# A seven-product output projection on one Trainium2 core: side work tied to the matmuls, and the two-group product moved to the end

## The chip, the cores and the metric

The kernel runs on one core of a Trainium2 chip. The metric is device microseconds of one execution, the median of several. The engines are named as the profile names them: PE (matmuls) and PEld (its weight loads), DVE (the vector engine), ACT (the scalar engine), POOL (GpSimd) and SP (which only starts transfers). A name with a q (SPq, ACTq) is the engine's instruction queue. Each engine executes its own list of instructions strictly in the order in which the program was laid out, and waits at an instruction whose inputs are not there yet.

## The reference, cut to what matters

One step of a layer with two kinds of attention heads, for 1024 prompt frames and 8 x 16 sample frames. All is float32.

```python
h = rms_norm(x, norm_pre)
q_sb, k_sb, v_sb, gate_sb, q_r, k_r, v_r, gate_r = project(h, w_in, pos)   # 2048 -> 8 x 1024
o_sb = stick_breaking_block(q_sb, k_sb, v_sb)        # 8 heads, strictly causal
o_r  = retention(q_r, k_r, v_r)                      # 8 heads, chunks of 64
y   = concat(head_norm(o_sb) * silu(gate_sb), head_norm(o_r) * silu(gate_r))
out = einsum('bte,ed->btd', y, w_out)                # 2048 x 2048
x   = x + rms_norm(out, norm_post)
```

## The kernel before, in words

**Precision.** A float32 matmul is made of three passes over operands that are split in a high part (rounded, by ACT) and a low part (the rest, by DVE). The helper `split` (L163) does that: L164 is its ACT instruction, L165 its DVE instruction. Weights go this way too: `wr` (as loaded) becomes `wh` and `wl`, 128 x 512 at a time. There are 5 buffers of `wr` and 4 of each half, so the splitting can run a few tiles ahead of PE.

**Order.** The program is written as nested loops over products, and between the matmuls `tick()` runs one step of one of a list of waiting generators (`Job`). A generator says with each `yield` how many ticks must pass before its next step. That fixes a program order. A scheduler then lays out each engine's list: it may pull an instruction ahead of the place where it was written when its model of the machine sees the engine free and the inputs ready. A helper `tied` (L186) keeps some instructions of the attention from being pulled ahead of the last projection matmul written before them (`anchor`): it adds a dependency that only the scheduler sees, with no wait on the chip.

**Stage 1 and 2.** The rows are handled in two groups: group 0 is four prompt tiles of 128 frames and the sample tile, group 1 the other four prompt tiles. For each group the kernel projects head after head (matmuls at L338 and L394, weights loaded at L327 and L380), and the attention of earlier heads runs between these matmuls. In the stick-breaking attention the weight rows `kp` and `be` of a tile go through a scan (L618), a product (L619), a turn through device memory (`s_be`), and a block transpose on DVE (L679), before PE multiplies them with the values (L719).

**The output projection** follows a seven-product scheme (Strassen's in Winograd's form) with 2 x 2 blocks of `w_out` and of `y`. Some products need sums of blocks. The function `sums` (L259) makes them: it loads a block of 4 x 256 columns into `br` (two buffers; two transfers, L249 or L257), does four DVE instructions (L274), and stores it from the ACT queue (L277), as `s_b` for the weights (32 items) and as `s_s` for the rows (8 items for each group). Between the steps of an item stand 4, 4, 4, 4 + 6 and 36 ticks, and the load of an item is written one whole item ahead. The 32 weight items and the 8 items of group 0's rows are started in group 1's first head, and are drained near its end; the rows of group 1 follow in the third stage.

**Stage 3.** `product(n, nh, groups, sample, ticks)` multiplies the left operand `mine[g, n]` of each group g by one half (nh) of the right block n: for each of 8 k it loads and splits a weight tile (L1142) and does three matmuls (L1127, L1128, L1129) for each accumulator `a`, two accumulators (tiles of 128 frames) a group. `left` (L282) prepares an operand: per k a load `yr` and a split into `mh`, `ml` (group 0) or `ah`, `al` (group 1). `collect` (L1179, L1181, L1177) adds a finished product to the areas `mh2`, `ml2`, `mh3`, `ml3` (group 0) and `out0` to `out3` (group 1) by the table GOES. An entry with a 1 at its end completes a block: `complete` then squares it (ACT, L1223) and multiplies it by `gpost` (DVE, L1230). After its four blocks a tile is finished by `finish`: the residual rows `xr` are loaded (L1243), the scale is computed (L236, L172 to L178: small DVE instructions and one square root on ACT), and each 512 columns are scaled and added (DVE at L1253, or ACT at L1250 and POOL at L1251) and stored (L1256).

The products before are, in this order: 5 and 3 for group 0 and the sample; 1, 2, 6, 7, 4 for both groups; 5 and 3 for group 1 alone. The last half product (3, group 1) is cut: the last 5 of its 8 k are multiplied tile after tile, from kept weights `mh2`, `ml2` (L1318), so that the first tile's finishing can start under the second tile's matmuls.

Of the kernel before, what the change touches and what calls it, by code (L numbers as in the profile page):

```python
# [16 lines left out]
P = 128  # L17
# [57 lines left out]
        1: ((C21, None, "+", 0),), 2: ((C11, C21, "+", 1),), 6: ((C12, C21, "+", 0),), 7: ((C22, C12, "+", 0),),  # L75
        4: ((C21, C22, "-", 1),), 5: ((C22, C22, "+", 1), (C12, C12, "+", 0)), 3: ((C12, C12, "+", 1),),
# [14 lines left out]
def tile_hybrid_step(  # L91
# [71 lines left out]
    def split(hi, lo, src):  # L163
        nc.scalar.activation(hi, src, AF.Copy)  # L164
        nc.vector.tensor_tensor(lo, src, hi.bitcast(F32), ALU.subtract)  # L165

    def inv_rms(pool, ssq, n, name):
# [11 lines left out]
        return r  # L179

# [62 lines left out]
    def sum_weights(k, c):  # L243
        cs = slice(c * 256, (c + 1) * 256)

        def load(r):
            for kk in range(2):
                rows = w_out[0, (kk * HT + k) * P : (kk * HT + k + 1) * P, :]
                nc.sync.dma_start(r[:, 2 * kk : 2 * kk + 2], rows.rearrange("p (a n) -> p a n", a=2)[:, :, cs])  # L249
# [4 lines left out]
    def sum_rows(gi, h):  # L254
        def load(r):
            for kk in range(2):
                nc.sync.dma_start(r[:, 2 * kk : 2 * kk + 2].rearrange("p a n -> p (a n)"), s_y[gi][kk * H + h][:, :512])  # L257
# [4 lines left out]
    def sums(pool, items):  # L262
# [8 lines left out]
        for i, (_, ops, dst) in enumerate(items):  # L271
            nxt = fetch(items[i + 1][0]) if i + 1 < len(items) else None
            for o, a, b, how in ops:
                nc.vector.tensor_tensor(r[:, o], r[:, a], r[:, b], ALU.add if how == "a" else ALU.subtract)  # L274
                yield D_SUM2[0]
            yield D_SUM2[1]
            nc.scalar.dma_start(dst, r)  # L277
# [3 lines left out]
    def left(gi, n, hi, lo, bufs, tag, deep):  # L281
# [3 lines left out]
        def load(h):  # L285
            r = bufs.tile([P, 256], F32, name=tag, tag=tag, bufs=deep)
            if src[0] == "y":
                nc.sync.dma_start(r, s_y[gi][src[1] * H + h][:, src[2] * 256 : src[2] * 256 + 256])
            else:
                nc.sync.dma_start(r, s_s[gi][h][:, src[1], :])  # L290
# [5 lines left out]
        for h in range(HT):  # L296
# [3 lines left out]
            split(hi[:, h], lo[:, h], r)  # L300
            yield D_OP

    def left_sample(kk, hi, lo, bufs, tag, deep):
        raw = []

        def load(h):
            r = bufs.tile([P, P], F32, name=tag, tag=tag, bufs=deep)
            nc.sync.dma_start(r, s_y[0][kk * H + h][:, 4 * P : 5 * P])
# [5 lines left out]
        for h in range(HT):  # L314
            if h + deep - 1 < HT:
                load(h + deep - 1)
            split(hi[:, h], lo[:, h], raw.pop(0))
# [90 lines left out]
    with ExitStack() as s1:  # L408
# [716 lines left out]
        def times(a, x, k, ts, wh, wl, first, last):  # L1125
# [3 lines left out]
            nc.tensor.matmul(a, lo[:, k, ts], wh, start=False, stop=last)  # L1129
# [69 lines left out]
    with ExitStack() as s3:  # L1199
# [5 lines left out]
        for c in range(4):  # L1205
            nc.scalar.dma_start(
                gpost[:, c * 512 : (c + 1) * 512], norm_post[0, c * 512 : (c + 1) * 512].partition_broadcast(P)
            )
# [10 lines left out]
        def square(key, c, o):  # L1219
# [3 lines left out]
            nc.scalar.activation(sq, o, AF.Square, accum_out=ssqs[key][0][:, c : c + 1])  # L1223
            ssqs[key][1].append(c)

        def complete(key, c):
# [3 lines left out]
            nc.vector.tensor_tensor(o, o, gpost[:, c * 512 : (c + 1) * 512], ALU.mult)  # L1230
# [8 lines left out]
        def load_rows(key):  # L1239
            xr = []  # L1240
            for a in range(2):
                xr.append(xp[0].tile([P, HALF], F32, name="xr", tag="xr", bufs=4))
                nc.sync.dma_start(xr[a], x_rows(tile_of(key))[:, a * HALF : (a + 1) * HALF])  # L1243
            return xr

        def scaled(key, c, rs, xr, pool, o=None):
            o = area(key, c) if o is None else o
            x = xr[c // 2][:, (c % 2) * 512 : (c % 2 + 1) * 512]
            if pool:
                nc.scalar.activation(o, o, AF.Copy, scale=rs)  # L1250
                nc.gpsimd.tensor_tensor(o, o, x, ALU.add)  # L1251
            else:
                nc.vector.scalar_tensor_tensor(o, o, rs, x, ALU.mult, ALU.add)  # L1253
# [17 lines left out]
        def both(n, i):  # L1271
            jobs_of = []
            mine[0, n] = operand(mp, (f"mh{i % 2}", f"ml{i % 2}"), 256)
            mine[1, n] = operand(c3, ("ah", "al"), 256, bufs=2)
            return [Job(left(g, n, *mine[g, n], rp, "yr", 4), D_OP) for g in (0, 1)]

        ready = [Job(left_sample(kk, *mine["s", kk], fp, "ys", 4), 1) for kk in (1, 0)]
        Job(collect(3, 0, product(3, 0, (0,), False, 1)), 1)
        for job in ready:
            drain(job)  # L1280
        ready = both(1, 0)
        Job(collect(3, 1, product(3, 1, (0,), True, 1)), 1)
        Job(collect(3, 0, product(3, 0, (), True, 2)), 1)
# [159 lines left out]
```

## Time and profile before

| | |
|---|---|
| median of 3 runs | 2404.86 us (2402.67 to 2405.93) |
| the profiled execution: its time | 2398.02 us |
| its span | 2396.3 us |
| PE busy | 2287.5 us (95%) |
| DVE, ACT, POOL busy | 1262.3, 927.8, 365.3 us |
| mean granted clock of PE | 0.984 |
| sums (L274) run | from 1177.7 us, until group 0's and the weights' are done near 1491 us |
| stage 3, first matmul to last | 1994.4 to 2376.0 us |

Matmuls are pipelined: one of 128 x 512 shows 0.39 us, but they start 0.23 us apart. PE's busy time therefore hides short waits, and the count of matmuls in a stretch of time says more. "Idle" in a row is the time in which an engine stood before that instruction, and the name behind the arrow is what ended it.

### The profile page before, as it was taken

How to read it: one execution, taken by the hardware profiler on the slowest of the kernel's cores; microseconds unless marked ns; L12 is line 12 of the kernel's file. 1: busy time of each engine (PE TensorE's matmuls, PEld its weight loads, DVE VectorE, ACT ScalarE, POOL GpSimd, SP SyncE). 2: the span in 40 equal slices, each digit the busy share in tenths (PEclk: the TensorE clock that was granted, in tenths of full speed). 3: DMA queues.
4: the chain of work that ended last, by engine and by line, in shares of the span. 5: the costliest groups of instructions: out<-in, count | busy, mean ns of one | idle time of the engine just before them, and what ended most of it. 6: DMA issues, size and time to landing. Idle time of an engine off the chain costs nothing. (4 is left out here: it accounts for less than half of the span.)

```text
span 2396.3 us, 39509 instructions
## 1 busy us (share of the span) xinstructions
PE 2287.5 (95%) x14496; PEld 2053.5 (86%) x14496; DVE 1262.3 (53%) x2580; ACT 927.8 (39%) x1968; POOL 365.3 (15%) x590
## 2 busy tenths in 40 slices
PE   7999999999999999999987979999999999899995
PEld 7999999999999999998876858888888887688884
DVE  7235444443535443455556565555454556655767
ACT  6324333333333333334332323343344445533443
POOL 3002020301112120202020201120211311000102
PEclk9999999999999999999998989999999999999998
DMA  7546666575756656776788888645555556774747
GB/s 249 192 145 177 191 177 200 168 220 157 215 177 183 197 148 191 200 234 206 221 257 249 253 248 260 160 134 153 156 150 145 159 155 163 247 244 159 240 135 251
DMA packets 448194, 465.24 MB, mean 194 GB/s; under 512 B 182144, under 2 KB 311168, under 8 KB 446848
## 3 DMA queue, kind: packets, MB, share of 16 engines
q1 hardware_dynamic: 321568, 305.92, 43.5%
q10 hardware_dynamic: 101344, 85.48, 11.0%
q0 software_dynamic: 25088, 71.33, 9.9%
q8 instruction: 113, 1.85, 0.3%
q14 instruction: 81, 0.66, 0.1%
HBM read 357.74 MB, written 104.86 MB: 193 GB/s over the span
## 5 line engine op out<-in xcount | busy, mean ns | idle before, releaser
L338 PE MATMUL acc<-mh,wl 128*128 128x256 f32 (+2 forms) x2304 | 659.0, 339 | 11.0 <-DVE wl L165 11.0
L338 PE MATMUL acc<-mh,wh 128*128 128x256 f32 (+2 forms) x2304 | 664.9, 341 | 0.8 <-DVE rk L431 0.7
L338 PE MATMUL acc<-ml,wh 128*128 128x256 f32 (+2 forms) x2304 | 663.3, 341 | 0.0
L165 DVE TENSOR_TENSOR wl<-wr,wh 128x512 fp32r<-128x512 f32 x531 | 366.7, 695 | 458.0 <-ACT wh L164 438.6
L164 ACT ACTIVATE wh<-wr 128x512 fp32r<-128x512 f32 x531 | 332.0, 630 | 660.4 <-PE acc L338 296.4
L338 PEld LDWEIGHTS acc<-mh,wl 128*128 128x128 f32 x2304 | 425.7, 189 | 41.1 <-DVE wl L165 13.6
L338 PEld LDWEIGHTS acc<-mh,wh 128*128 128x128 f32 x2304 | 421.6, 189 | 34.4 <-issue 3.3
L338 PEld LDWEIGHTS acc<-ml,wh 128*128 128x128 f32 x2304 | 423.3, 189 | 31.3 <-issue 3.3
L394 PE MATMUL accn<-whn,mh 128*128 128x256 f32 x1152 | 330.1, 287 | 0.0
L394 PE MATMUL accn<-wln,mh 128*128 128x256 f32 x1152 | 326.2, 283 | 0.3 <-DVE wln L165 0.3
L394 PE MATMUL accn<-whn,ml 128*128 128x256 f32 x1152 | 325.6, 283 | 0.0
L394 PEld LDWEIGHTS accn<-whn,mh 128*128 128x128 f32 x1152 | 221.0, 192 | 3.4 <-issue 1.1
L394 PEld LDWEIGHTS accn<-wln,mh 128*128 128x128 f32 x1152 | 221.1, 192 | 1.3 <-DVE wln L165 0.5
L394 PEld LDWEIGHTS accn<-whn,ml 128*128 128x128 f32 x1152 | 220.8, 192 | 0.0
L165 DVE TENSOR_TENSOR wln<-wrn,whn 128x512 fp32r<-128x512 f32 x128 | 88.0, 689 | 146.2 <-ACT whn L164 145.8
L164 ACT ACTIVATE whn<-wrn 128x512 fp32r<-128x512 f32 x128 | 80.7, 633 | 189.9 <-PE accn L394 87.7
L274 DVE TENSOR_TENSOR br<-br 128x256 f32<-128x256 f32 x192 | 79.0, 423 | 106.6 <-DMA br<-w_out 72.7
L582 POOL DMA_DIRECT2D be<-s_be x128 | 94.1, 742 | 133.7 <-DMA s_be<-be 115.1
L607 POOL TENSOR_SCALAR_AFFINE_SELECT kb<-kb 128x128 f32<-128x128 f32 x64 | 30.7, 488 | 455.7 <-ACT kb L601 453.5
L618 DVE TENSOR_TENSOR_SCAN kp<-kp 128x1152 f32<-128x1152 f32 (+4 forms) x40 | 82.3, 2058 | 33.4 <-POOL kp L607 16.8
L745 POOL DMA_DIRECT2D kcT<-cache_k x64 | 34.9, 547 | 422.6 <-PE pd L822 268.5
L1127 PE MATMUL a<-wh,mh 128*128 128x512 f32 x224 | 88.2, 399 | 7.9 <-ACT wh L164 7.9
(230 smaller groups left out, 3053.1 us busy)
## 6 DMA issues: line engine op xcount, KB each, us to landing
wr<-w_cols SPq DMA_DIRECT2D x384, 256.0 KB, 3.9
wrn<-w_rows SPq DMA_DIRECT2D x128, 256.0 KB, 3.2
kcT<-cache_k POOLq DMA_DIRECT2D x64, 512.0 KB, 8.0
vc<-cache_v SPq DMA_DIRECT2D x64, 512.0 KB, 5.5
wr<-s_b SPq DMA_DIRECT2D x80, 256.0 KB, 3.5
wr<-w_out SPq DMA_DIRECT2D x72, 256.0 KB, 4.3
br<-w_out SPq DMA_DIRECT2D x64, 256.0 KB, 5.2
s_b<-br ACTq DMA_DIRECT2D x32, 512.0 KB, 5.2
```

The source lines that it names most:

```text
L164: nc.scalar.activation(hi, src, AF.Copy)
L165: nc.vector.tensor_tensor(lo, src, hi.bitcast(F32), ALU.subtract)
L274: nc.vector.tensor_tensor(r[:, o], r[:, a], r[:, b], ALU.add if how == "a" else ALU.subtract)
L338: last = nc.tensor.matmul(a[:, :m], lhs[:, j, :], rhs[w][:, j, o : o + m], start=(w == 0 and j == 0 and n == 0), stop=(w == KT // WQ - 1 a ...
L394: anchor[0] = nc.tensor.matmul(a, lhs[q][:, jj, ts], rhs[:, j, :], start=(w == 0 and j == 0 and n == 0 and t % 2 == 0), stop=(w == KT // 2 ...
L582: q.dma_start(raw[32 * i : 32 * i + 32, :].rearrange("p (k a) -> p k a", a=32), s[:, :, 32 * i : 32 * i + 32].rearrange("k (j b) a -> b (k ...
L607: nc.gpsimd.affine_select(blk, blk, pattern=[[-1, P]], base=0, channel_multiplier=1, compare_op=ALU.is_gt, fill=fill,)
L618: nc.vector.tensor_tensor_scan(rev, rev, rev, 1.0, ALU.mult, ALU.bypass)
L745: ready.append((kc, nc.gpsimd.dma_start(kc, cache_k[h, m // 4, m % 4])))
L1127: nc.tensor.matmul(a, hi[:, k, ts], wh, start=first, stop=False)
```

## The change

- A new helper `pin` does for any instruction what `tied` does, in all stages: the scheduler may not lay it out ahead of the matmul last written. It is put on the loads, DVE instructions and stores of `sums`, on the loads and splits of `left` and `left_sample`, and in stage 3 on squares, the multiplication by `gpost`, the loads of `xr` and the DVE and ACT part of the scaling. The matmuls of `times` in stage 3 now set `anchor`, so the pins follow them. The loads and splits of weights, the additions of `collect` and the small instructions of the scale are not pinned.
- `gpost` is loaded from POOL's queue by a generator in place of ACT's queue at the start of stage 3.
- The products' order is 5 and 3 (group 0, sample), 1, 2, 6, 7 (both), 5 and 3 (group 1), then 4 (both). GOES for group 1 follows: product 7 now also writes C21, and 4 subtracts from C21. That adds four DVE additions of 128 x 512.
- The cut last half product is now that of 4 with its four accumulators: four tiles are finished at the end, two of each group, in place of two. `og` has two buffers in place of one, `xr` six in place of four; in this tail one of four column blocks of a tile goes by ACT and POOL, as before.
- The sample's operands are prepared at two places (one ahead of each half of product 3) in place of both at once.

```diff
     1: {
-        1: ((C21, None, "+", 0),), 2: ((C11, C21, "+", 1),), 6: ((C12, C21, "+", 0),), 7: ((C22, C12, "+", 0),),
-        4: ((C21, C22, "-", 1),), 5: ((C22, C22, "+", 1), (C12, C12, "+", 0)), 3: ((C12, C12, "+", 1),),
+        1: ((C21, None, "+", 0),), 2: ((C11, C21, "+", 1),), 6: ((C12, C21, "+", 0),),
+        7: ((C22, C12, "+", 0), (C21, C12, "+", 0)), 4: ((C21, C21, "-", 1),), 5: ((C22, C22, "+", 1), (C12, C12, "+", 0)), 3: ((C12, C12, "+", 1),),
     },
...
+    def pin(*made):
+        if anchor[0] is not None:
+            for ins in made:
+                tc.add_manual_dep(
+                    ins.ins,
+                    anchor[0].ins.name,
+                    mybir.DependencyInfo(mybir.DependencyClass.NoSync, mybir.DependencyReason.SCHED_ONLY),
+                    reason="not ahead of the products",
+                )
...
             for o, a, b, how in ops:
-                nc.vector.tensor_tensor(r[:, o], r[:, a], r[:, b], ALU.add if how == "a" else ALU.subtract)
+                pin(nc.vector.tensor_tensor(r[:, o], r[:, a], r[:, b], ALU.add if how == "a" else ALU.subtract))
                 yield D_SUM2[0]
             yield D_SUM2[1]
-            nc.scalar.dma_start(dst, r)
+            pin(nc.scalar.dma_start(dst, r))
...
             r = raw.pop(0)
-            split(hi[:, h], lo[:, h], r)
+            pin(*split(hi[:, h], lo[:, h], r))
             yield D_OP
...
-            nc.tensor.matmul(a, lo[:, k, ts], wh, start=False, stop=last)
+            anchor[0] = nc.tensor.matmul(a, lo[:, k, ts], wh, start=False, stop=last)
...
+        then = {1: (2, (0, 1), 1), 2: (6, (0, 1), 0), 6: (7, (0, 1), 1), 7: (5, (1,)), 5: (3, (1,)), 3: (4, (0, 1), 0)}
+        for n, groups in ((1, (0, 1)), (2, (0, 1)), (6, (0, 1)), (7, (0, 1)), (5, (1,)), (3, (1,))):
+            all_of(ready)
+            if n == 2:
+                drain(more)
+            ready = both(*then[n])
             for nh in range(2):
-                accs = product(n, nh, (0, 1), n < 3, 1)
+                accs = product(n, nh, groups, n < 3, 1)
...
+        all_of(ready)
+        Job(collect(4, 0, product(4, 0, (0, 1), False, 1)), 1)
...
-        accs = product(3, 1, (1,), False, 1, HT - KEPT)
+        accs = product(4, 1, (0, 1), False, 1, HT - KEPT)
...
-        rows = [load_rows((1, p)) for p in range(2)]
-        for p, (_, a) in enumerate(accs):
-            key = 1, p
+        rows = {}
+        for i, ((g, p), a) in enumerate(accs):
+            key = g, 2 + p
...
+            for j in range(i, min(i + 2, 4)):
+                g1, p1 = accs[j][0]
+                if j not in rows:
+                    rows[j] = load_rows((g1, 2 + p1))
```

How the lists of instructions change is shown at three places. Numbers behind a name tell buffers apart; a line number of the changed kernel is some 12 to 17 higher than that of the same statement before.

**DVE, group 1's attention, around the transpose of one tile (kp_14549).** `wln` and `wl` are weight halves, `br` the sums. Before:

```order
L274 TENSOR_TENSOR br_16569<-br_16569 128x256 x4
L165 TENSOR_TENSOR wln_14772<-wrn_14769,whn_14771 128x512
L165 TENSOR_TENSOR wln_14802<-wrn_14799,whn_14801 128x512
L274 TENSOR_TENSOR br_16720<-br_16720 128x256 x2
L618 SCALAR_TENSOR_TENSOR kp_14676<-kp_14676 128x768
L165 TENSOR_TENSOR wln_14834<-wrn_14831,whn_14833 128x512
L619 TENSOR_TENSOR be_14677<-be_14677,kp_14676 128x768
L679 STREAM_TRANSPOSE kp_14549<-be_14550 128x640
L274 TENSOR_TENSOR br_16720<-br_16720 128x256
```

With the change:

```order
L286 TENSOR_TENSOR br_14489<-br_14489 128x256 x2
L166 TENSOR_TENSOR wln_14772<-wrn_14769,whn_14771 128x512
L286 TENSOR_TENSOR br_14489<-br_14489 128x256 x2
L166 TENSOR_TENSOR wln_14802<-wrn_14799,whn_14801 128x512
L166 TENSOR_TENSOR wln_14834<-wrn_14831,whn_14833 128x512
L630 SCALAR_TENSOR_TENSOR kp_14676<-kp_14676 128x768
L631 TENSOR_TENSOR be_14677<-be_14677,kp_14676 128x768
L691 STREAM_TRANSPOSE kp_14549<-be_14550 128x640
L166 TENSOR_TENSOR wln_14890<-wrn_14887,whn_14889 128x512
```

By this place the list before has come to the item with buffer 16569, the changed one to 14489, twelve items earlier: the sums are spread over almost all heads of group 1.

**SP, the loads of `br` among those of the weights in group 1.** Before:

```order
L327 DMA wr_13905<-w_cols 128x512
L249 DMA br_14034<-w_out 128x2x256 x2
L327 DMA wr_13935<-w_cols 128x512
L249 DMA br_14186<-w_out 128x2x256 x2
L327 DMA wr_13979<-w_cols 128x512
L249 DMA br_14352<-w_out 128x2x256 x2
L327 DMA wr_14005<-w_cols 128x512
```

With the change:

```order
L339 DMA wr_13905<-w_cols 128x512
L339 DMA wr_13935<-w_cols 128x512
L261 DMA br_13703<-w_out 128x2x256 x2
L339 DMA wr_13979<-w_cols 128x512
L339 DMA wr_14005<-w_cols 128x512
L339 DMA wr_14039<-w_cols 128x512
L339 DMA wr_14065<-w_cols 128x512
L339 DMA wr_14095<-w_cols 128x512
L261 DMA br_13876<-w_out 128x2x256 x2
```

One item's two loads stood behind each weight tile; now they stand behind each fifth or so.

**DVE, from group 1's product 3 to what follows it.** Before, the last half product and the finishing of a tile (`outr`, `outu`):

```order
L165 TENSOR_TENSOR wl3_24412<-wr3_24409,wh3_24411 128x512
L1179 TENSOR_TENSOR out1_21802<-out1_21802,a3_24265 128x512
L165 TENSOR_TENSOR wl3_24426<-wr3_24423,wh3_24425 128x512
L174 RECIPROCAL outr_24438<-outr_24438 128x1
L165 TENSOR_TENSOR ml2_24389<-wr3_24447,mh2_24388 128x512
L175 TENSOR_TENSOR outu_24439<-outr_24438 128x1
```

With the change the same product is followed by 4, whose operands `ml0` and `al` are prepared here:

```order
L166 TENSOR_TENSOR wl3_24068<-wr3_24065,wh3_24067 128x512
L166 TENSOR_TENSOR al_23835<-yr_23941,ah_23834 128x256
L166 TENSOR_TENSOR wl3_24083<-wr3_24080,wh3_24082 128x512
L166 TENSOR_TENSOR wl3_24097<-wr3_24094,wh3_24096 128x512
L166 TENSOR_TENSOR ml0_23833<-yr_23969,mh0_23832 128x256
L166 TENSOR_TENSOR wl3_24123<-wr3_24120,wh3_24122 128x512
L166 TENSOR_TENSOR al_23835<-yr_23976,ah_23834 128x256
L1245 TENSOR_TENSOR out0_21795<-out0_21795,gpost_21358 128x512
```

The row with `wr3_24120` is the first weight tile of product 4; the operands' last k stand behind it.

More of the change, by code (lines that the diff above doesn't have):

```diff
@@ L307, in load @@
             r = bufs.tile([P, P], F32, name=tag, tag=tag, bufs=deep)
-            nc.sync.dma_start(r, s_y[0][kk * H + h][:, 4 * P : 5 * P])
+            pin(nc.sync.dma_start(r, s_y[0][kk * H + h][:, 4 * P : 5 * P]))
             raw.append(r)
@@ L316, in left_sample @@
                 load(h + deep - 1)
-            split(hi[:, h], lo[:, h], raw.pop(0))
+            pin(*split(hi[:, h], lo[:, h], raw.pop(0)))
             yield D_OP
@@ L1204, in tile_hybrid_step, with load_gpost @@
         gpost = c3.tile([P, D], F32, name="gpost")
[L1205 to L1208, printed above, removed]
+        def load_gpost():
+            for c in range(4):
+                cs = slice(c * 512, (c + 1) * 512)
+                pin(nc.gpsimd.dma_start(gpost[:, cs], norm_post[0, cs].partition_broadcast(P)))
+                yield 8
         phases = ExitStack()
@@ L1229, in complete @@
             yield D_FIN
-            nc.vector.tensor_tensor(o, o, gpost[:, c * 512 : (c + 1) * 512], ALU.mult)
+            pin(nc.vector.tensor_tensor(o, o, gpost[:, c * 512 : (c + 1) * 512], ALU.mult))
             if len(ssqs[key][1]) == 4:
@@ L1241, in load_rows @@
             for a in range(2):
-                xr.append(xp[0].tile([P, HALF], F32, name="xr", tag="xr", bufs=4))
-                nc.sync.dma_start(xr[a], x_rows(tile_of(key))[:, a * HALF : (a + 1) * HALF])
+                xr.append(xp[0].tile([P, HALF], F32, name="xr", tag="xr", bufs=6))
+                pin(nc.sync.dma_start(xr[a], x_rows(tile_of(key))[:, a * HALF : (a + 1) * HALF]))
             return xr
@@ L1269, in finish, with both, all_of @@
             store(key, 3, nc.scalar)
[L1271 to L1277, printed above, removed]
+        def both(n, groups, i=0):
+            made = []
+            for g in groups:
+                if g == 0:
+                    mine[0, n] = operand(mp, (f"mh{i % 2}", f"ml{i % 2}"), 256)
+                else:
+                    mine[1, n] = operand(c3, ("ah", "al"), 256, bufs=2)
+                made.append(Job(left(g, n, *mine[g, n], rp, "yr", 4), 1))
+            return made
+        def all_of(made):
+            for job in made:
+                drain(job)
+        ready = [Job(left_sample(1, *mine["s", 1], fp, "ys", 4), 1)]
         Job(collect(3, 0, product(3, 0, (0,), False, 1)), 1)
-        for job in ready:
-            drain(job)
-        ready = both(1, 0)
+        all_of(ready)
+        ready = both(1, (0, 1), 0)
         Job(collect(3, 1, product(3, 1, (0,), True, 1)), 1)
+        ready.append(Job(left_sample(0, *mine["s", 0], fp, "ys", 4), 1))
         Job(collect(3, 0, product(3, 0, (), True, 2)), 1)
```

67 lines of the change are left out of this document (26 added, 41 removed).

## The prediction

> **What bounds the kernel now.** I read the page's head first, then the busy time by stretches, then the waits of PE and of the engines that feed it, then the order of time at one stall and at the end.
>
> ```profile
> span 2396.3 us, 39509 instructions
> PE 2287.5 (95%) x14496; PEld 2053.5 (86%) x14496; DVE 1262.3 (53%) x2580; ACT 927.8 (39%) x1968; POOL 365.3 (15%) x590
> 1180.00:1500.00 320.00, 278.04 (x1535) 240.31 (x1534) 190.45 (x395) 100.55 (x212) 46.20 (x73) 0.94 0.85 254
> 1520.00:1920.00 400.00, 396.42 (x2284) 348.16 (x2282) 212.62 (x378) 159.89 (x338) 74.49 (x113) 1.00 0.54 148
> 1990.00:2090.00 100.00, 88.72 (x373) 68.68 (x372) 58.83 (x129) 54.05 (x120) 2.18 (x3) 0.95 0.69 204
> 2190.00:2290.00 100.00, 100.00 (x443) 82.80 (x442) 75.29 (x146) 48.35 (x112) 9.60 (x6) 1.00 0.71 228
> 2345.00:2376.00 31.00, 25.74 (x97) 18.40 (x95) 25.75 (x50) 13.67 (x30) 6.42 (x4) 0.94 0.75 250
> 2376.00:2396.30 20.30, 0.00 (x0) 0.00 (x0) 10.54 (x29) 4.56 (x10) 6.47 (x4) 0.63 0.75 276
> ```
>
> Columns of the stretches: from and to, length, busy time and count of PE, PEld, DVE, ACT, POOL, then PE's granted clock, the share of DMA and GB/s. PE bounds the kernel, and the change removes none of its work; what can be won are the places where it stands. The counts show them. Group 1's later heads start 2284 matmuls in 400 us, 5.71 per us; the stretch from 1180 to 1500, of the same kind of work, only 1535 where 320 x 5.71 = 1827 were due: short by 292, or **51 us**. In stage 3 the full rate is 443 per 100 us; from 1990 to 2090 there are 373, short by 70 or **16 us**, and from 2345 to 2376 97 of 137, short by 40 or **9 us**. After the last matmul **20.3 us** pass.
>
> The first stretch is that of the sums:
>
> ```profile
> L274 DVE TENSOR_TENSOR br<-br x192: 382/424/519, 1177.7 to 2135.6; 128x256 f32<-128x256 f32 x192
> L277 ACTq DMA_DIRECT2D s_b<-br x32: 520/521/788, 1183.1 to 1491.3; - x32
> DMA to landing us min/median/max: 2.5/5.1/10.9
> DVE br L274 <- DMA br<-w_out: 72.7, 36, 7.9
> DVE br L274 <- DMA br<-s_y: 15.1, 6, 6.3
> ACT wh L164 <- DVE br L274: 53.8, 8, 9.2
> PE pa L719 <- DVE kp L679: 29.5, 5, 11.9
> PE acc L338 <- DVE wl L165: 11.0, 6, 3.9
> ```
>
> The first three rows tell when the sums run and how long their instructions and transfers take, the others who waited between 1170 and 1520 (total, times, longest). DVE stood 88 us for loads of `br`; ACT's queue stood behind stores that wait for these sums; and PE waited for what DVE had behind them. One case in order of time:
>
> ```profile
> 1260.74 8.04 SPq L327 DMA_DIRECT2D wr<-w_cols  x3
> 1264.32 0.89 DVE L274 TENSOR_TENSOR br<-br 128x256 f32<-128x256 f32 x2 [4.33 <-DMA br<-s_y]
> 1268.31 0.63 ACT L164 ACTIVATE wh<-wr 128x512 fp32r<-128x512 f32 x1 [7.97 <-DVE br L274]
> 1272.00 1.11 DVE L679 STREAM_TRANSPOSE kp<-be 128x896 f32<-128x896 f32 x1
> 1273.16 3.14 PE L719 MATMUL pa<-vn,kp 128*128 128x128 f32 x13 [11.47 <-DVE kp L679]
> ```
>
> The transpose stands in DVE's list behind sums whose rows were not there; PE idles 11.5 us.
>
> **The change part by part.**
>
> *Sums in group 1's heads.* Nothing is removed: 160 instructions of 0.424 us (68 us of DVE), 40 stores and 80 loads remain, and the order shows them spread over nearly all heads. An item has 4 x 4 + 6 + 36 = 58 ticks and a matmul of the projections gives about one, so the 40 items take at least 2320 / 5.71 = 406 us in place of the 314 us between 1177 and 1491; some ticks go to other generators, so I expect about 650. Then each load is written a whole item ahead, at least 58 / 5.71 = 10 us, against a median landing of 5.1 us: DVE no longer waits for it. What stays is load: DVE was at 212.62 / 400 = 53% in the later heads, and 68 us in 650 add 10 points. DMA there moves 148 GB/s; the sums move 40 items of 0.5 MB twice, 40 MB in 650 us or 62 GB/s, together 210. Group 0 shows that this much does no harm:
>
> ```profile
> 980.00:1080.00 100.00, 100.00 (x734) 96.08 (x733) 53.83 (x115) 37.77 (x87) 20.23 (x38) 1.00 0.71 210
> PE pa L719 <- DVE kp L679: 2.7, 3, 1.1
> ```
>
> (The second row: PE's waits for the transpose from 1520 to 1920, in heads without sums.) Of the 51 us I let 5 remain, for sums that stand ahead of a transpose with their data present: **-46**. Bounds: -51 if all is hidden, -25 if half the stall comes from DVE being fuller (60% busy in that stretch) and not from the loads.
>
> *Front of stage 3.* The waits of PE from 1990 to 2090 are for split weights:
>
> ```profile
> PE a L1127 <- ACT wh L164: 8.2, 5, 4.9
> 2018.62 8.23 SPq L1142 DMA_DIRECT2D wr<-w_out  x5
> DMA packets 6899, 12.94 MB, mean 259 GB/s; under 512 B 769, under 2 KB 2218, under 8 KB 6896
> ```
>
> With pins, the sample's and product 1's operands no longer come ahead of weight tiles in ACT's and DVE's lists, and half of the sample's work moves one product back. But the data stay: three half products of 8 weight tiles (6.3 MB), 16 row loads of 128 KB and 16 of 64 KB (3.1 MB) make 9.4 MB. At 259 GB/s (the third row: 2090 to 2140, the densest stretch here) that is 36 us, against 144 matmuls at 4.43 per us, 32.5 us. At least 4 us stay; I let 8 stay: **-8**, bounds -14 and 0.
>
> *Sums of group 1's rows, before product 6.* Here the pins bunch: 8 items take 464 ticks, product 1 offers 80, and the rest is written behind its last matmul. The list puts the last six items across half of product 2, on two buffers.
>
> ```profile
> DVE br L274 <- DMA br<-s_y: 16.1, 5, 5.5
> PE a L1128 <- DVE wl L165: 0.6, 1, 0.6
> ```
>
> Before, the same bunch (2097 to 2137) cost DVE 16.1 us of waiting and PE 0.6 (second row, 2090 to 2290), since five accumulators make a weight tile last 15 / 4.43 = 3.4 us. Six items at a load and a store of about 5 us each on two buffers take 30 us and more, where the list leaves 24: **+2**, bounds 0 and +8.
>
> *Products 5 and 3 with one group, now ahead of 4.* A weight tile feeds only 6 matmuls there, 1.35 us. DVE's costs:
>
> ```profile
> L165 DVE TENSOR_TENSOR wl<-wr,wh 128x512 fp32r<-128x512 f32 x145 | 102.3, 714 | 90.2 <-ACT wh L164 87.7 <-DMA wr<-s_b 1.3 <-DMA yr<-s_y 0.7
> L165 DVE TENSOR_TENSOR ml<-yr,mh 128x256 fp32r<-128x256 f32 x40 | 16.7, 420 | 2.4 <-ACT mh L164 2.4
> L1179 DVE TENSOR_TENSOR out<-out,a 128x512 f32<-128x512 f32 x26 | 17.4, 680 | 0.1
> 2322.00:2345.00 23.00, 23.00 (x104) 18.98 (x102) 21.92 (x46) 16.12 (x38) 3.02 (x2) 1.00 0.58 184
> ```
>
> In product 5 the list has 16 `wl`, 8 operand halves and 15 additions and multiplications: 16 x 0.71 + 8 x 0.42 + 15 x 0.68 = 25.0 us, where PE needs 96 / 4.43 = 21.7. In product 3 it is 16, 11 and 9: 22.1 us. The four added additions (2.7 us) are in these numbers. The excess of 3.3 us is covered by the tiles split ahead (product 7 is light), as before: the last row is the old place of product 5, with DVE 21.92 of 23 us busy and PE at full rate. The 9 us lost after it came from product 3 with finishing of four tiles, their `xr` and their stores around it; now its neighbour is product 4, which needs a weight tile only each 2.7 us. But its four loads of `xr` (512 KB each) stand ahead of product 4's last weights on SP. I let 5 of the 9 stay: **-4**, bounds -9 and +8 (the 2 MB at 250 GB/s, if no weight is ahead).
>
> *The end.* Four tiles in place of two are finished behind the last products:
>
> ```profile
> 2375.61 0.39 PE L1129 MATMUL a<-mh,al 128*128 128x512 f32 x1
> 2378.34 0.68 DVE L1329 TENSOR_TENSOR out<-out,a 128x512 f32<-128x512 f32 x1
> 2388.55 0.72 ACT L1250 ACTIVATE out<-out,outr 128x512 f32<-128x512 f32 x1 [1.00 <-DVE outr L178]
> 2391.45 0.69 DVE L1332 TENSOR_TENSOR og<-out,gpost 128x512 f32<-128x512 f32 x1 [1.49 <-DMA out<-og]
> 2392.96 0.34 ACTq L1256 DMA_DIRECT2D out<-og  x1
> L1253 DVE SCALAR_TENSOR_TENSOR out<-out,outr,xr x8: 736/748/1772, 2372.4 to 2389.2; 128x512 f32<-128x512 f32 x8
> 2377.74 1.74 POOL L1251 TENSOR_TENSOR out<-out,xr 128x512 f32<-128x512 f32 x1 [4.07 <-ACT out L1250]
> ```
>
> Before, the second tile's subtraction starts 2.3 us after the last matmul, and its `og` waits until the first's store has read the one buffer. Two buffers take that away. One tile costs DVE 0.68 + 0.69 + 7 small ones of 0.16 + 3 x 0.75 = 4.7 us, four 18.8. The first tile is ready 3 x 15 / 4.43 = 10.2 us ahead of the last matmul. From there: a square root's round by ACT (about 1 us), 18.8 us of DVE, 2 us of finishing left over from product 4's first half, and up to 1 us for each of four POOL additions (rows 6 and 7: a scaling beside one took 1.77 in place of 0.75); the last store takes 2396.3 - 2392.96 = 3.3. That is 10.2 us less: 15 to 19 after the last matmul, 16.5 taken: **-4**. Bounds: -8, if tiles overlap in ACT's rounds as well, and +4, if 6 MB of stores and `xr` at 276 GB/s (22 us) decide.
>
> On those POOL additions the Trainium skill (SBUF — State Buffer, "SBUF: two separate sides") has a rule against the change: a DVE instruction with two SBUF inputs and a GpSimd one that reads SBUF lock each other out for a whole instruction. The 1.77 us agrees in kind, though it is 1.0 and not 1.74 us longer. By the full lock the four additions of 1.74 us would add 7 us in place of at most 4, the end would be 22 us long, and the sum 54 in place of 60.
>
> `gpost` from POOL's queue costs nothing: the queue is empty from 1995 on, and the first use stands in product 1's second half.
>
> Sum: -46 - 8 + 2 - 4 - 4 = **-60 us**. On the profiled execution's own time, 2398.0, this is 2338; that execution is 6.8 us below the median of the runs, so I add the 6.8: **2345 us**.
>
> **The rivals.**
>
> *Half the stall stays.* If the stall from 1180 to 1500 is DVE being full and the heads' chains being long, spreading only thins it: 25 of the 51 stay, and the time is about 2368. For it: DVE is only 60% busy there against 53 later. Against it: 88 us of DVE's waits carry the name of `br`'s loads.
>
> *All of it goes.* Nothing of the sums is left, the front of stage 3 loses its 4 us of bandwidth alone, the end shrinks by 8: -51 - 12 - 9 - 8, about 2325.
>
> *Slower: SP is held by the sums' buffers.* The load of an item needs the buffer that was stored one item before, and the store is issued only 36 / 5.71 = 6.3 us ahead of it. If the store has not landed, SP stands, and all weight loads behind it. Landing goes up to 10.9 us, so a hold of 4.6 us is seen possible. PE has five tiles of `wr` of 12 matmuls, 12 / 4.43 = 2.7 us each, so only a hold beyond 13 us reaches it. 40 such holds of 15 us would give back 80 us of stalls where 51 go away, and with the rest about 2418. It decides from landings of about 20 us on; none is in the trace.
>
> *The change does nothing on the chip*, since a pin is a wish to the scheduler: the lists do differ, so only the losses in stage 3 could cancel the gain. About 2405.
>
> **How the numbers follow.** Forecast (2332 to 2360) 0.57; half the stall 0.16; all of it 0.15; slower 0.06; no change 0.03; the rest lies between these. The range holds the forecast and most of its two neighbours: 2322 to 2382. A difference under 0.2% (5 us) can't be told from none here. Faster 0.91, same 0.03, slower 0.06.
>
> **What would show it.** In the profile after: between 1180 and 1500 the rate of matmuls near 5.7 per us and the clock at 1.00; sums running until about 1830; PE's waits for the transposes near 1 us each; no long wait of DVE for `br` before stage 3. The last matmul some 56 us earlier, and 16 to 17 us between it and the end. The forecast is wrong if the rate stays under 5.4 all through group 1, if the one-group products 5 and 3 lose over 8 us, or if the end grows beyond 20 us.

## The result and the profile after

| | before | with the change |
|---|---|---|
| median | 2404.35 us of 4 runs (2402.67 to 2405.93) | 2333.78 us of 4 runs (2329.52 to 2336.49) |
| ratio of the times | | 0.9705 (95% interval 0.9688 to 0.9722) |
| the profiled execution | 2398.02 us | 2334.38 us |
| its span | 2396.3 us | 2332.7 us |
| last matmul to the end | 20.3 us | 22.6 us |

The change is 70.6 us faster by the medians, where 60 were forecast (2345 us). The time lies 11 us under the forecast and inside its range. The heads of the page and the stretches of the changed kernel, with the columns of the stretches shown before:

```profile
span 2332.7 us, 39504 instructions
PE 2269.9 (97%) x14496; PEld 2045.1 (88%) x14496; DVE 1266.4 (54%) x2586; ACT 926.0 (40%) x1964; POOL 362.7 (16%) x592
1180.00:1500.00 320.00, 316.90 (x1810) 277.08 (x1803) 195.66 (x387) 126.77 (x270) 53.53 (x84) 1.00 0.74 208
1520.00:1920.00 400.00, 395.38 (x2261) 346.36 (x2260) 240.63 (x438) 159.85 (x327) 80.00 (x123) 1.00 0.71 202
1930.00:2030.00 100.00, 92.55 (x413) 72.13 (x412) 65.36 (x141) 52.08 (x128) 7.51 (x11) 0.98 0.75 213
2223.40:2266.80 43.40, 43.40 (x194) 35.93 (x193) 39.13 (x73) 29.51 (x67) 0.00 (x0) 1.00 0.79 237
2266.80:2310.10 43.30, 43.30 (x190) 35.12 (x188) 30.48 (x63) 18.65 (x40) 7.67 (x5) 1.00 0.71 227
2310.10:2332.70 22.60, 0.04 (x1) 0.00 (x0) 16.02 (x37) 4.94 (x12) 5.30 (x4) 0.56 0.89 279
```

From 1180 to 1500 PE now starts 1810 matmuls in place of 1535 and has its full clock; the row of the later heads lost only 23 of 2284 although the sums now run there too. From 1930 to 2030, where the front of stage 3 now lies, PE starts 413 matmuls; in the 100 us of that front shown before, from 1990 on, it was 373. The sixth and seventh rows are products 5 and 3 of group 1 and then product 4: 194 and 190 matmuls in 43.4 us, the full rate of 4.43 per us. The last row is the end. The next rows show the sums by the view of their tile (the first four), who waited between 1170 and 1520 (the fifth), and who waited between 1930 and 2200, in stage 3 (the last):

```profile
L286 DVE TENSOR_TENSOR br<-br x192: 380/420/552, 1193.6 to 2116.2; 128x256 f32<-128x256 f32 x192
L261 SPq DMA_DIRECT2D br<-w_out x64: 550/602/1719, 1184.8 to 1858.1; - x64
L289 ACTq DMA_DIRECT2D s_b<-br x32: 520/521/562, 1201.1 to 1881.8; - x32
DMA to landing us min/median/max: 2.6/4.2/7.6
PE pa L731 <- DVE kp L691: 3.1, 3, 1.1
DVE br L286 <- DMA br<-s_y: 9.9, 4, 4.0
```

The sums take 697 us of the heads (1184.8 to 1881.8) in place of 314. DVE no longer waits for loads of `br` in any head; its only waits for it, 9.9 us, are in stage 3, ahead of product 6. PE waits for the transposes 3.1 us in place of 29.5.

Where the time went is read best from the same matmul in both traces: the n-th of a kind before, less the n-th now. The columns are the profiled execution of the change and one of a repeat of it (label e8_again, 2333.02 us, ratio 0.9713, 0.9695 to 0.9732); each number is worked out from the starts of the matmuls. (In the last three products, whose order differs, it is the n-th matmul counted from the end.)

| stretch, by the time before | change | repeat |
|---|---|---|
| up to the start of group 1's projections (1120.6) | -6.2 | -2.8 |
| from there to 1545, the sums | +56.4 | +56.5 |
| later heads, to 1994 (stage 3 begins) | +0.3 | +0.3 |
| front of stage 3, to 2100 | +6.3 | +3.5 |
| from there to 2277, where product 7 ends | +0.3 | -0.5 |
| the last three products | +8.8 | +8.1 |
| last matmul to the end | -2.3 | -2.8 |
| span | +63.6 | +62.3 |

### The profile page after: what moved, and what is told of

Same layout as the page of the kernel before. It is cut to its first block, busy times and chain, and to the rows that moved or that the text cites. A ratio compares the mean times of both kernels' runs of the same rounds, so it can differ in the third digit from the quotient of the medians.

```text
span 2332.7 us, 39504 instructions
## 1 busy us (share of the span) xinstructions
PE 2269.9 (97%) x14496; PEld 2045.1 (88%) x14496; DVE 1266.4 (54%) x2586; ACT 926.0 (40%) x1964; POOL 362.7 (16%) x592
## 4 chain that ended last, share of the span: by engine, by line
PE 83%; DMA 7%; DVE 5%; issue 2%; ACT 2%; SPq 1%; POOL 0%; DVEq 0%; ACTq 0%; POOLq 0%
PE acc L350 46%; PE accn L406 17%; PE a L1140 3%; PE a L1141 3%; PE a L1139 3%; PE pa L731 3%; PE z L701 2%; PE zc L770 1%; PE pd L834 1%; DMA mr<-s_h 1%; DMA dT<-c_dt 1%; DMA yr<-s_y 1%; DVE kp L630 1%; PE pa L879 1%; DMA wr<-w_out 1%
## 5 line engine op out<-in xcount | busy, mean ns | idle before, releaser
L286 DVE TENSOR_TENSOR br<-br 128x256 f32<-128x256 f32 x192 | 80.6, 420 | 13.5 <-DMA br<-s_y 9.9
```

Of the source, the lines that this page charges most:

```text
L286: pin(nc.vector.tensor_tensor(r[:, o], r[:, a], r[:, b], ALU.add if how == "a" else ALU.subtract))
```

## The experiments

### The sums alone, and all but the sums

My theory: the stall is sums laid out ahead of their data, and the pins on four statements of `sums` take it away. The rival: DVE is full there, and only a part goes. The first kernel is the one before with `pin` on the two loads, the DVE instruction and the store of `sums` (the cut shows the last two); the second is the changed one without these four.

```diff
-                nc.vector.tensor_tensor(r[:, o], r[:, a], r[:, b], ALU.add if how == "a" else ALU.subtract)
+                pin(nc.vector.tensor_tensor(r[:, o], r[:, a], r[:, b], ALU.add if how == "a" else ALU.subtract))
...
-            nc.scalar.dma_start(dst, r)
+            pin(nc.scalar.dma_start(dst, r))
```

> The kernel before, with the pins on the loads, DVE instructions and stores of the sums alone; stage 3, its order and its end stay. Theory (the stall of group 1 came from sums laid out ahead of their data): the matmuls from 1120 to 1545 us gain 50 to 57 us as they did in the change, the rest stays, so the median falls from 2404 to about 2351 (2346 to 2358). Rival (half the stall is a fuller DVE, or the gain needs the other pins too): 2370 or more.

> The changed kernel without the pins on the sums; everything else of the change stays. Theory: the stall from 1180 to 1500 comes back nearly whole, 50 us or more, and the gains of stage 3 stay (17 us at the front and in the products, 2 lost at the end): about 2388 (2380 to 2395). Rival (the pins of the operands and the new order carry much of the gain): 2370 or less.

Measured: 2349.54 us with the sums' pins alone, ratio 0.9779 (0.9763 to 0.9796), and 2391.45 without them, 0.9951 (0.9934 to 0.9967). The stretch from 1180 to 1500, of the first and then of the second kernel:

```profile
1180.00:1500.00 320.00, 316.90 (x1800) 277.39 (x1799) 194.62 (x383) 124.75 (x263) 53.39 (x84) 1.00 0.74 210
```

```profile
1180.00:1500.00 320.00, 275.16 (x1508) 237.93 (x1507) 186.60 (x391) 97.31 (x203) 44.27 (x69) 0.93 0.84 249
```

And the waits of the second between 1170 and 1520:

```profile
DVE br L286 <- DMA br<-w_out: 75.0, 39, 8.0
ACT wh L165 <- DVE br L286: 49.5, 9, 8.5
PE pa L731 <- DVE kp L691: 29.7, 4, 12.5
PE acc L350 <- DVE wl L166: 11.1, 6, 4.2
```

By the same matmuls the first kernel gains 56.5 us to 1545, all that the change gains there; the second loses 4.6. The rows of the second are those of the kernel before (72.7, 53.8, 29.5 and 11.0 us). The theory holds, and both medians lie in the ranges given for it: four pinned statements carry the whole gain up to 1545, and the other pins have no share in it. Which of the four are needed was not tried. In the later heads, up to 1973, the first kernel then loses 5.1 us, where the change loses 0.9; whether that is the missing pins or this one execution isn't shown.

### Place or density

The pins do two things: no sum is laid out ahead of its place, and the ticks that the generator counts spread the items over 697 us. To tell these apart the ticks of an item were cut from 58 to 27, with all pins in place.

```diff
-D_SUM2 = (4, 6, 36)
+D_SUM2 = (2, 3, 16)
```

> The change with the waits between the steps of a sum item cut from 4, 6 and 36 ticks to 2, 3 and 16: 27 ticks an item in place of 58, pins kept, so the sums run in about half the stretch, some 320 us, as densely as before the change, but each load still an item ahead of its use. Theory (waiting for loads in the wrong place made the stall): at most 10 us slower than the change, 2334 to 2344. Rival (the density of DVE and DMA work made it): 20 us slower or more, 2354 and up.

Measured: 2341.16 us, ratio 0.9737 (0.9719 to 0.9756). The sums of the heads run from 1177.0 to 1518.6 there, 342 us, nearly as densely as before the change (314 us). The stretch and the waits between 1170 and 1520:

```profile
1180.00:1500.00 320.00, 305.40 (x1718) 268.12 (x1716) 209.40 (x413) 114.07 (x234) 55.57 (x84) 0.98 0.90 261
```

```profile
DVE br L286 <- DMA br<-w_out: 27.6, 20, 5.4
POOL s_be L587 <- DVE br L286: 27.4, 4, 10.5
PE pa L731 <- DVE kp L691: 13.5, 4, 5.8
```

Here DMA is at 0.90 and DVE waits again for `br`, 27.6 us where it had been 72.7; PE pays 13.5 us at the transposes. To 1545 this execution gains 38.6 us where the change gains 56.4: about two thirds of the gain come with the place alone, and 18 us need the thinner spacing. By 1973, when the change too has its sums behind it, it is 41.6 of 55.5 us, so 14 us, a quarter, are left to the spacing. By the medians the density costs only 7 to 8 us. In the profiled execution that is because the matmul at 1120.6 started 7.7 us earlier than in the change's, with the same instructions up to there, and because the end is 2.8 us shorter; whether the other executions, which have no trace, are like it stays open.

### The order of the products

The changed kernel with all its pins, but with the old order, table, tail and four buffers of `xr`, and with the sample's operands prepared at once as before:

```diff
-        then = {1: (2, (0, 1), 1), 2: (6, (0, 1), 0), 6: (7, (0, 1), 1), 7: (5, (1,)), 5: (3, (1,)), 3: (4, (0, 1), 0)}
+        seq = (1, 2, 6, 7, 4)
...
-        accs = product(4, 1, (0, 1), False, 1, HT - KEPT)
+        accs = product(3, 1, (1,), False, 1, HT - KEPT)
```

> All pins of the change, but the order of the products, the table of additions, the cut last product with two tiles and the buffers of the residual rows as before. Theory (the order wins some 7 us in products 5 and 3 and loses some 2 at the end): 5 us slower than the change, about 2339 (2335 to 2343). Rival (the pins alone won the 7 us, and four tiles at the end cost more than two): 2334 or less, with under 20 us between the last matmul and the end.

Measured: 2347.06 us, ratio 0.9763 (0.9743 to 0.9782). The order, with what was put back beside it, is worth 13 us, not 5, and not nothing: a miss of both expectations. Its last 54 us of matmuls:

```profile
2273.00:2296.00 23.00, 19.86 (x80) 15.73 (x79) 17.86 (x37) 13.42 (x30) 1.07 (x1) 0.93 0.79 264
2296.00:2327.00 31.00, 23.30 (x89) 17.16 (x88) 22.97 (x48) 14.15 (x29) 7.78 (x6) 0.94 0.81 258
```

and who waited there (2280 to 2350):

```profile
DVE wl L166 <- ACT wh L165: 7.5, 4, 3.6
PE a L1139 <- ACT wh L165: 6.6, 2, 3.5
PE a L1139 <- ACT mh L165: 2.6, 1, 2.6
```

At 4.43 per us 102 and 137 matmuls were due: 22 and 48 are missing, 16 us. With the old order the one-group products stand beside the finishing of tiles and wait for weights that ACT splits late. The kernel before lost 9 us there. By the matmuls counted from the end, the old order with the sums' pins alone loses 2 us more than that, with all pins 6.7. Which of the other pins does it was not tried.

The other half of the question, the new order without any pin (`pin` does nothing):

```diff
-        if anchor[0] is not None:
+        if False:
```

> The change with no pin at all: new order, its end, gpost from POOL's queue. Theory (pins on the sums win some 52, those of the operands and the row finishing with the new order 10 to 13): the stall of group 1 as before, and the scheduler free to bring operands and finishing forward: 2388 to 2400. Rival (the pins outside the sums win nothing, the order does it all): as the change without pins on the sums, 2391 or less.

Measured: 2395.57 us, ratio 0.9985 (0.997 to 1.0001), inside the theory's range. Its ten runs lie between 2393.9 and 2409.1 us. Without the pins the new order brings 6 us by the medians and 3.6 by the ratio, whose interval just includes no gain at all; with the pins it is 13. The kernel without the sums' pins alone stands at 2391.45, so the other pins bring some 4 us by the medians where the sums are not held.

### The end

The end grew by 2.3 us where 3.8 less were forecast, so six runs ask what sets it. The first takes ACT and POOL out of it, and so the slow scaling beside a POOL addition:

```diff
-                scaled(key, c, rs, rows[i], c == 2)
+                scaled(key, c, rs, rows[i], False)
```

> The change with all four column blocks of the last four tiles scaled and added by DVE; nothing goes by ACT and POOL there. Theory (each POOL addition makes a DVE instruction beside it 1.0 us longer): four times 1.0 us less and four times 0.74 us more on DVE, so 0 to 3 us faster than the change. Rival (the POOL additions are free, and DVE is the bound at the end): 3 us slower, DVE having four more instructions.

Measured: 2332.7 us, ratio 0.9709 (0.969 to 0.9728), the repeat of the change in the same runs 2333.02: no difference that can be told, where the theory had 0 to 3 us less and the rival 3 more. The end is 22.1 us. What evens out there is worked out further down, with the POOL additions. The second keeps all 8 k of the last half product in SBUF, so that the first tile is ready 3 x 24 / 4.43 = 16.3 us ahead of the last matmul in place of 10.2:

```diff
-        accs = product(4, 1, (0, 1), False, 1, HT - KEPT)
+        accs = product(4, 1, (0, 1), False, 1, 0)
...
-            for k in range(KEPT):
+            for k, (kh, kl) in enumerate(kept):
```

> The change with all 8 k of the last half product multiplied tile after tile, the other 3 kept weights in the buffers mh1 and ml1, which product 7 has left. A tile then has 24 matmuls, 5.4 us of PE, in place of 15 and 3.4. Theory (the end is four tiles of some 5 us of DVE each behind 3.4 us of PE each, and a backlog of 5 us): DVE keeps up with PE, the end shrinks from 22.6 to 12 to 15 us after the last matmul, 2324 to 2328. Rival (transfers of 8 MB of rows and results set the end): 2331 or more.

Measured: 2333.39 us, ratio 0.9706 (0.9679 to 0.9733), with an end of 21.9 us. Its first and last subtraction (the last matmul ends at 2311.2):

```profile
2301.22 0.67 DVE L1348 TENSOR_TENSOR mh<-mh,a 128x512 f32<-128x512 f32 x1
2322.18 0.67 DVE L1348 TENSOR_TENSOR out<-out,a 128x512 f32<-128x512 f32 x1
```

DVE begins 10 us ahead of the last matmul where it is 5 with the change, but then needs 21 us to come to the fourth tile. The earlier start bought nothing that can be told. The theory (2324 to 2328) missed; the time is where the rival put it, but whether transfers are the cause, as it had it, this run doesn't show. Then transfers and DVE's work were taken out in turn: one tile's residual rows for all four, and three of four blocks stored unscaled. Both kernels leave out work that the result needs.

```diff
-            for j in range(i, min(i + 2, 4)):
-                g1, p1 = accs[j][0]
-                if j not in rows:
-                    rows[j] = load_rows((g1, 2 + p1))
+            if i == 0:
+                rows[0] = load_rows((g, 2 + p))
+            rows[i] = rows[0]
```

> The change, but the four last tiles all use the residual rows of the first of them: three loads of 1 MB are left out, so three tiles get the wrong residual; DVE, ACT, POOL and the stores do the same work. Theory A (transfers set the end: 6.3 MB at 274 GB/s after the last matmul, and the last tile's rows are asked for only when the first tile's buffers are free): the end of 22 to 23 us falls to about 17, and the time from 2333 to 2327 to 2329. Theory B (DVE's chain of four tiles sets the end): 2332 to 2334, since not one DVE instruction goes away.

```diff
             for c in (2, 0, 3):
-                scaled(key, c, rs, rows[i], c == 2)
                 store(key, c, nc.sync)
```

> The change, but in the four last tiles the column blocks 0, 2 and 3 are stored without being scaled and without the residual (left out: 8 DVE instructions of 0.75 us, some of them 1.75, and 4 each of ACT and POOL); all loads and stores stay, and stores can be issued sooner. Theory B (DVE's chain): 8 DVE instructions with their slow ones make 8 to 10 us, the end falls to about 14, the time to 2324 to 2326. Theory A (transfers): the end stays at 20 us or more, the time at 2330 to 2333, for the 6.3 MB have to pass in any case.

Measured: 2330.64 us, 0.97 (0.9672 to 0.9729), and 2330.12 us, 0.9694 (0.9664 to 0.9724). By time neither can be told from the change. With one tile's rows theory A had an end of 17 us and theory B a time of 2332 to 2334; neither came. Without the scaling theory B had an end of 14 us and theory A one of 20 or more; it is 18.7, at a time inside A's range. Their profiles tell more. The end with one tile's rows:

```profile
2304.90:2325.90 21.00, 0.04 (x1) 0.00 (x0) 15.69 (x36) 4.72 (x12) 5.45 (x4) 0.62 0.54 188
2299.46 0.68 DVE L1345 TENSOR_TENSOR mh<-mh,a 128x512 f32<-128x512 f32 x1
2319.68 1.75 DVE L1268 SCALAR_TENSOR_TENSOR og<-og,outr,xr 128x512 f32<-128x512 f32 x1
```

and without the scaling:

```profile
2308.40:2327.10 18.70, 0.00 (x0) 0.00 (x0) 9.05 (x30) 2.06 (x7) 0.00 (x0) 0.59 0.65 250
2309.73 0.75 DVE L1268 SCALAR_TENSOR_TENSOR og<-og,outr,xr 128x512 f32<-128x512 f32 x1 [2.85 <-DMA xr<-x_prompt]
2317.21 0.69 DVE L1349 TENSOR_TENSOR og<-out,gpost 128x512 f32<-128x512 f32 x1 [2.65 <-DMA out<-og]
```

In the first, DMA is at 0.54 and waits for work, and yet DVE's chain from the first tile's subtraction to the last scaling takes 22.0 us (2299.46 to 2319.68 + 1.75): the end is only 1.6 us shorter. In the second, DVE is at 9.05 us, and it stands for `xr` and for the buffer `og` to be stored: 3.9 us shorter. I read this as two limits of nearly the same length, DVE's chain and the transfers, where taking one away shows the other. It rests on one profiled execution of each kernel. Last, with nothing left out, the third and fourth tile's rows were loaded ahead, into free space, with and without POOL in the tail:

```diff
+            if i < 2:
+                rows[i] = load_rows((g, 2 + p))
+            else:
+                xt = mp.tile([P, D], F32, name="xt3", tag=("mh1", "ml1")[i - 2])
+                rows[i] = [xt[:, a * HALF : (a + 1) * HALF] for a in range(2)]
```

> The change, with nothing left out: all residual rows of the four last tiles are loaded before the first of them is multiplied, the third and fourth tile's into the free space of mh1 and ml1, so that they don't wait for buffers. Theory A: 2 MB move from after the last matmul to before it, where DMA stands at 0.74; the end falls by 3 to 5 us and the time to 2328 to 2331, unless PE loses it again to weights that come later. Theory B: 2332 to 2334; only the 1.2 us that DVE's last tile stands for its rows go away.

> The kernel with the early rows, and in the last four tiles no scaling by ACT and POOL: DVE does all four blocks of 0.75 us (4 x 0.75 = 3.0 us more on DVE, and 4 x 1.0 less where a scaling beside a POOL addition takes 1.75). Alone, that changed the time by less than 1 us. Theory A (transfers hid it): with the rows early DVE's chain decides, the last tile saves POOL's 1.8 us and the time is 1 to 2 us under the early rows alone. Theory B: the same within 1 us, as before.

Measured: 2335.69 us, 0.9726 (0.9697 to 0.9756), and 2334.41 us, 0.9719 (0.9694 to 0.9744): no gain by either. The first is slower than both theories had it; the second is 1.3 us under the first, as its first theory said, but the runs of both spread over 6 us and more, so that can't be told. The rows of the first for the 14.5 us ahead of the last matmul, for the end, and of one instruction in it:

```profile
2292.00:2306.50 14.50, 14.50 (x65) 11.70 (x63) 13.08 (x26) 5.90 (x14) 6.11 (x4) 1.00 0.92 278
2306.50:2333.20 26.70, 0.04 (x1) 0.00 (x0) 16.68 (x37) 4.94 (x12) 5.65 (x4) 0.56 0.61 213
2314.70 0.69 DVE L1353 TENSOR_TENSOR og<-out,gpost 128x512 f32<-128x512 f32 x1 [4.76 <-DMA out<-og]
```

The rows now fill DMA (0.92) just when the first tile is to be stored; its store lands late, `og` is not free, and DVE stands 4.76 us. The end is 26.7 us, 4.1 longer than with the change (24.7 us without POOL): the wait was shifted, not won. No kernel here is faster than the change beyond what can be measured.

## Why the prediction was right, and where it was wrong

The sum was made on the profiled execution of before, which was 6.8 us under its median; that of the change is 0.6 above its own. Between the two spans lie 63.6 us, but 6.2 us of them were lost up to 1120.6, ahead of anything that the change moves. Without these it is 69.8, which the terms are held against. (Two times of rivals were added up loosely: by the prediction's own terms half the stall gives 2365, not 2368, and the slower rival 2420, not 2418.)

| term | forecast (bounds) | measured |
|---|---|---|
| sums in group 1's heads, with the later heads | -46 (-51 to -25) | -55.5 |
| front of stage 3 | -8 (-14 to 0) | -7.5 |
| bunched sums ahead of product 6 | +2 (0 to +8) | about 0 |
| one-group products ahead of product 4 | -4 (-9 to +8) | -8.8 |
| the end | -4 (-8 to +4) | +2.3 |
| sum | -60 | -69.5 |

The measured column is the first column of the table above, its later heads put to the sums for the 0.9 us that they lost to 1973 and to the front for the rest; 0.3 us of products 1 to 7 is left out. That the time came within 11 us of the forecast is in part luck: the sums and the products won 14 us more than forecast, the end came out 6 us worse, and these errors partly cancel. One of the prediction's own signs of being wrong came true: the end grew beyond 20 us.

**The sums.** The mechanism is as said: the rate is 1810 / 320 = 5.66 per us, the clock 1.00, DVE has no wait for `br` in the heads, PE's waits for the transposes are at most 1.1 us, and DMA in the later heads carries 202 GB/s where 210 were worked out; DVE is there at 240.63 / 400 = 60%, 7 points above the 53% of before, where 10 had been added. The sums end at 1882, not 1830. The step that failed is the size of the stall, "short by 292, or 51 us", and its upper bound. I took the stretch to end at 1500 with the sums, but 3.3 of the 56.4 us come from the 45 us after it, and the matmuls of that stretch run denser without the stall than the later heads, from whose rate I counted: its 1535 matmuls now take 320 - 53.2 = 266.8 us, 5.75 per us in place of 5.71. And of the 5 us left for sums ahead of a transpose next to nothing remained. The density run shows that this depends on the spacing: at 27 ticks 18 us remain up to 1545.

**The rival of half the stall** had DVE's load as its cause. It falls with the run with the sums' pins alone, where DVE is as busy from 1180 to 1500 as before (194.62 against 190.45 us) and the whole 56.5 us are won. **The rival in which all of it goes** (2325) is nearer to the measured time than the forecast (9 us against 11): its sums (51) and products (9) came, the sums with more than that; its end, 8 us shorter, did not. **The slower rival**, SP held by a store of sums, is not in the trace: between 1180 and 1900 SP stood 0.5 us in all ahead of loads of `br` from `w_out`, and these landed within 7.6 us, where the rival needed about 20.

**The front of stage 3** gave what was taken. Counted the same way, from 1973 to 2100, the gain lies between 3.6 and 8.8 us in the repeat and in the six kernels that differ from the change only in the end, so the exact 7.5 is luck.

**Products 5 and 3.** The direction holds (the two rows at full rate), but I let 5 of the 9 us stay, for `xr` on SP ahead of product 4's weights. None stayed. The run with the old order shows the loss where the one-group product stands beside the finishing; and since that loss is larger with all pins, the order is worth some 13 us beside the pins and at most about 6 without them.

**The end** is the term with the wrong sign. Its working had three parts: DVE free 2 us after the first tile is ready, some 21 us of chain, 3.3 us for the last store. The rows of the changed kernel:

```profile
2299.55 0.39 PE L1141 MATMUL a<-mh,ml 128*128 128x512 f32 x1
2300.26 1.78 DVE L1245 TENSOR_TENSOR mh<-mh,gpost 128x512 f32<-128x512 f32 x1
2304.98 0.68 DVE L1346 TENSOR_TENSOR mh<-mh,a 128x512 f32<-128x512 f32 x1
2309.75 0.39 PE L1141 MATMUL a<-mh,al 128*128 128x512 f32 x1
2324.88 0.75 DVE L1268 SCALAR_TENSOR_TENSOR out<-out,outr,xr 128x512 f32<-128x512 f32 x1 [1.16 <-DMA xr<-x_prompt]
2326.21 1.82 DVE L1268 SCALAR_TENSOR_TENSOR out<-out,outr,xr 128x512 f32<-128x512 f32 x1
2326.22 1.26 POOL L1266 TENSOR_TENSOR out<-out,xr 128x512 f32<-128x512 f32 x1 [4.50 <-DMA xr<-x_prompt]
```

The first tile is ready at 2299.9, as worked out, but DVE begins with it at 2305.0: 5.0 us later, not 2, for it has the finishing and the multiplications of product 4's first half in front. The chain takes 23.05 us (2304.98 to 2328.03). The last store lands 4.7 us after it, not 3.3. That is 3 + 1.7 + 1.4, the 6.1 us between 16.5 and 22.6. The backlog alone doesn't decide, though: with all weights kept DVE began 5 us earlier, and the end was as long.

**The POOL additions.** The prediction took up to 1 us for each of the four, and weighed a rule by which it would be 7 us for all. One addition and the scaling beside it are the last two rows above. Here is another such pair, behind a subtraction:

```profile
2309.44 0.68 DVE L1346 TENSOR_TENSOR ml<-ml,a 128x512 f32<-128x512 f32 x1
2315.25 1.73 POOL L1266 TENSOR_TENSOR ml<-ml,xr 128x512 f32<-128x512 f32 x1 [4.58 <-ACT ml L1265]
2315.78 1.75 DVE L1268 SCALAR_TENSOR_TENSOR og<-og,outr,xr 128x512 f32<-128x512 f32 x1
```

The scaling ends at 2317.53, 0.55 us after its addition (2316.98), and the one above at 2328.03, 0.55 us after its own (2327.48). So do all DVE instructions of 128 x 512 that are stretched beyond 0.85 us after 2000 us, 130 in the fourteen traces: each ends 0.54 to 0.56 us after a POOL addition. DVE stands until the addition is through, and it loses only what is left of the addition when it comes to it: the scalings beside the four additions took 1.18, 1.75, 1.75 and 1.82 us in place of 0.75, together 3.5 us more. POOL stands in its turn: an addition takes 1.26 us with no scaling beside it (the kernel before, at 2380.72) and 1.73 to 1.77 when it begins under one. The subtraction of the first row, which reads PE's accumulator `a`, ran inside an addition (2308.91 to 2310.66) without being stretched.

By the Trainium skill (SBUF — State Buffer, "SBUF: two separate sides"), a DVE instruction with two inputs in SBUF and a GpSimd one that reads SBUF don't share: the one that starts first has their shared port pair for its whole instruction, and the other waits. The trace agrees, and the prediction was wrong to read "1.0 and not 1.74 us longer" against it, and to count 4 x 1.74 = 7 us by it, for 1.74 us is more than DVE can lose to an addition of 1.26. The 22 us that it worked out for the end by that rule is near the 22.6 by chance; the end grew by the three sizes above. The sizes also fit that taking POOL out of the tail changed nothing: DVE is spared 3.5 us of standing and has four scalings more, at 0.67 us each in a row (2.08 us for three in that run's trace), 2.7 us; its chain there is 23.3 us (2304.47 to 2327.79).

## What to carry to other kernels

Where an engine stands for loads in the middle of a list that others wait on, look first at what was laid out ahead of its place: an in-order list makes one early instruction's wait everybody's. Hold side work to its place and then spread it over all the time there is; here the place was worth three quarters of the gain by the traces, and more than that by the times. And where one engine's chain and the transfers are about equally long, as they seem to be at this end, don't expect much from a single edit: six of them changed nothing that could be told. Read both lengths before costing one of them.

## What the runs showed of the hardware that was not expected

Equal lists of instructions did not run equally. In the stretch from 980 to 1080, ahead of all that differs (the lists part at about 1174 us, at the first load of `br`), the profiled execution before started 734 matmuls, and that of the change

```profile
980.00:1080.00 100.00, 97.46 (x704) 93.27 (x704) 49.74 (x108) 34.91 (x81) 17.09 (x31) 0.98 0.68 198
```

only 704; the repeat had 723. Over the profiled executions of the change and of the twelve runs, the matmul at 1120.6 started between 6.2 us later and 1.5 us earlier than before. One profile of each kernel is thus good to about 6 us here, and the same matmul in both traces shows which part of a difference is the edit's.

Transfers held 403 to 434 GB/s for 6.5 us with DMA's share near full, where I had taken 260 to 276 as the most, the means of the densest stretches of before (single slices of 1.25 us in them reached 423). The row is of the kernel without the scaling, its end in slices of 0.47 us:

```profile
GB/s 175 254 298 342 368 421 421 421 421 421 421 421 403 416 412 434 429 421 421 390 425 351 232 118 44 9 0 0 377 184 0 0 0 0 350 210 0 0 0 0
```

There the transfers that are issued are rows of `xr` and stores of the result. The change itself held 388 to 428 GB/s for the last 6 us before its transfers ran out. What lets these pass faster than the mix of before was not tried.
